# A decoder block's opening: x in rows with row sums of squares, the first modulation block shared by TensorE and VectorE, and the turned x loaded by pieces

## The chip, the core and the metric

The kernel runs on one core of a Trainium2 chip. The metric is the device time of one execution in microseconds (us). Five engines work side by side, each through its own instructions in a fixed order: TensorE (PE in the profile; its weight loads are PEld), VectorE (DVE), ScalarE (ACT), GpSimd (POOL) and SyncE (SP), which here only issues DMAs. An instruction that waits for another engine or for a DMA holds up everything behind it on its own engine.

## The reference

The reference is one decoder block on 256 rows of width 2048, in float32. Only its beginning matters here:

```python
ada = c @ w_ada + b_ada                      # c (1, 2048), w_ada (2048, 6144)
shift, scale, gate = jnp.split(ada, 3, axis=-1)
h = rms_norm(x, g_pre) * (1.0 + scale[:, None, :]) + shift[:, None, :]
proj = h @ w_in                              # w_in (2048, 11824)
```

`rms_norm` divides each row of x by the root of its mean square (plus 1e-6) and multiplies by g_pre. After that come two attention mixers on slices of `proj`, two branch products, a merge, an output product, a second norm with `gate`, and the residual sum. All of that is the same in both kernels.

## The kernel before

**The products.** Activations are kept turned: width on partitions, rows of x along the free axis. The width of 2048 falls into 16 blocks of 128, numbered kt. `h` is made piece by piece: block 0, blocks 1 to 2, 3 to 6, 7 to 9, 10 to 12 and 13 to 15. Pass 0 multiplies block 0 of h with its weights for 16 panels of `w_in` (8 items of two panels each, read in float32 by L564, the last two items by L560). Pass 1 takes blocks 1 and 2, pass 2 blocks 3 to 6, pass 3 the rest. From pass 1 on, a weight item is split into a high half `wH` (ACT, L520) and a low half `wL` (DVE, L521), and TensorE makes three products (L582, L584, L587).

**The modulation.** For block kt, shift and scale are sums of a column block of `w_ada` times c. `w_ss` holds those columns turned, so that output columns lie on partitions and the sum over the 2048 runs along the free axis. VectorE multiplies such a tile by `cB`, a copy of c on all partitions, and adds up along the row: L194 in eight halves for block 0, L529 in 1024-wide items for the others. `cB` is copied out of `c_ps`, four products of a column of ones with c in one row (L142).

**The norm.** `xs` holds the turned x (four DMAs of 512 KB). ACT squares it (L172, L179), GpSimd adds two halves (L173), VectorE squares a last part (L181), and TensorE sums over partitions with 40 matmul instructions on a column of ones (L186). From the sums, `rsqrt` makes `rstd`; L225 spreads it over all partitions into `rB_ps`, ACT copies that to `rstdB`. Block 0 is `x0` (L260), then `hF` (L283). GpSimd multiplies the other 15 blocks of `xs` by `rstdB` into `xT` (L751, five instructions), and `make_h` reads them.

**Order.** `items` is one list of weight items and modulation items. SP issues their DMAs in that order (`dma`, L501) into a ring of 7 buffers `raw`, each of 512 KB; a buffer is issued again once its reader is done. The first four buffers hold block 0's modulation weights. `keep_warm` (L135) issues matmuls whose results nobody reads. `behind` sets an instruction after another in the scheduler's order; the rest of each engine's order is the scheduler's, fixed when the kernel is built.

Of the kernel before, what the change touches and what calls it, by code (L numbers as in the profile page):

```python
# [9 lines left out]
F32 = mybir.dt.float32  # L10
# [40 lines left out]
def _build(ctx, tc, d_in, out):  # L51
# [39 lines left out]
    crow = ST[0:1, 2:4].rearrange("p a n -> p (a n)")  # L91
    pos_i = const.tile([128, 3], I32)
    A.dma_start(crow, d_in["c"])
    for q in range(4):
        DMA.dma_start(xs[:, 4 * q:4 * q + 4, :], d_in["xT"][:, 4 * q:4 * q + 4, :])
# [53 lines left out]
    i_mask = finish_mask_b()

    def c_halves():
        for j in (1, 3):
            last = A.activation(cB[:, j // 2, 512:1024], c_ps[j], AF.Copy)
        return last


    raws0 = []
    for q in range(4):
        r = wp.tile([128, 2, 512], F32, name="raw0", tag="raw", bufs=RAW)
        for half in range(2):  # L160
            DMA.dma_start(r[:, half], d_in["w_ss"][0, :, half, q * 512:(q + 1) * 512])
        raws0.append(r)

    last_sq = []
    ss_ps = psum.tile([128, NT, 2], F32, name="ss_ps", tag="pt")
    for q in range(4):
        if q % 2 == 0:
            sqs = big.tile([128, 2, 1024], F32, name="sqs", tag=("za", "zb")[q // 2])
        sq, xq = sqs[:, q % 2], xs[:, 4 * q:4 * q + 4, :].rearrange("p k s -> p (k s)")
        if q < 3:  # L170
            with behind(*last_sq):
                last_sq = [A.activation(sq, xq, AF.Square)]  # L172
            G.tensor_tensor(sq[:, 0:512], sq[:, 0:512], sq[:, 512:1024], op=OP.add)  # L173
            if q == 0:
                with behind(*last_sq):
                    last_sq = [c_halves()]
        else:
            with behind(*last_sq):
                A.activation(sq[:, 0:512], xq[:, 0:512], AF.Square)  # L179
            with behind(i_cV, i_mask):  # L180
                i_sq = V.tensor_tensor(sq[:, 512:1024], xq[:, 512:1024], xq[:, 512:1024], op=OP.mult)  # L181
        nk = 2 if q < 3 else 4
        for k in range(nk):
            for t in range(NT):
                with behind(i_warm):
                    i_ss = T.matmul(ss_ps[:, t, 0:1], lhsT=sq[:, k * S + t * 128:k * S + (t + 1) * 128],  # L186
                                    rhs=ones[:, 0:1], start=(q == 0 and k == 0 and t == 0),
                                    stop=(q == 3 and k == nk - 1), skip_group_check=True)
    sums0 = const.tile([128, 2, 5], F32)

    def sum0(q, half, after):
        r = raws0[q][:, half]
        with behind(after):
            return V.scalar_tensor_tensor(r, r, 1.0, cB[:, q // 2, q % 2 * 512:(q % 2 + 1) * 512], op0=OP.mult,  # L194
                                          op1=OP.mult, accum_out=sums0[:, half, q:q + 1])

    with behind(i_sq):
        V.tensor_copy(sums0[:, 0, 4:5], bT[:, 0, 0:1])
        i_sum = V.tensor_scalar(sums0[:, 1, 4:5], bT[:, 1, 0:1], 1.0, None, op0=OP.add)
    for q in range(2):  # L200
        for half in range(2):
            i_sum = sum0(q, half, i_sum)
    ssq = const.tile([128, NT], F32)
    with behind(i_sum):
        i_ssq = V.tensor_scalar(ssq, ss_ps[:, :, 0], 1.0 / D, EPS, op0=OP.mult, op1=OP.add)
    i_sum = sum0(2, 0, i_ssq)
# [16 lines left out]
    rB_ps = psum.tile([128, S], F32, name="rB_ps", tag="pv")  # L223
    for t in range(NT):
        i_rB = T.matmul(rB_ps[:, t * 128:(t + 1) * 128], lhsT=rstd[:, t:t + 1].to_broadcast([128, 128]), rhs=ident,  # L225
                        start=True, stop=True)
# [5 lines left out]
    A.activation(rstdB, rB_ps, AF.Copy)  # L232

# [26 lines left out]
    V.scalar_tensor_tensor(x0, xs[:, 0], gT[:, 0:1], rB_ps, op0=OP.mult, op1=OP.mult)  # L260

# [5 lines left out]
    def make_h(a, b):  # L267
        n = b - a
        if a:
            V.tensor_tensor(AB[:, :, a:b], sums[:, :, a:b, 0], bT[:, :, a:b], op=OP.add)  # L270
            V.tensor_tensor(AB[:, :, a:b], sums[:, :, a:b, 1], AB[:, :, a:b], op=OP.add)
            V.scalar_tensor_tensor(AB[:, 1, a:b], AB[:, 1, a:b], 1.0, gT[:, a:b], op0=OP.add, op1=OP.mult)
            h = ST[:, 2 + len(hxn) % 2].rearrange("p (k s) -> p k s", k=4)
        else:
            V.tensor_reduce(AB[:, :, 0], sums0, axis=AX.X, op=OP.add)
            h = hF
        hxn.append(a)
        for kt in range(a, b):
            src = xT[a][:, kt - a] if a else x0
            if a >= PASSES[2][0]:  # L280
                A.activation(h[:, kt - a], src, AF.Identity, scale=AB[:, 1, kt:kt + 1], bias=AB[:, 0, kt:kt + 1])
            else:
                V.tensor_scalar(h[:, kt - a], src, AB[:, 1, kt:kt + 1], AB[:, 0, kt:kt + 1], op0=OP.mult, op1=OP.add)  # L283
        ia = A.activation(xH[:, a:b], h[:, :n], AF.Copy)
        low = lows(a, b, "xL", F32R)
        iv = V.tensor_tensor(low, h[:, :n], xH[:, a:b].bitcast(F32), op=OP.subtract)
        xL.put(low, a, b)
        return ia, iv
# [143 lines left out]
    def ada_items(piece):  # L432
        a, b = piece
        res = []
        for kt in range(a, b):
            for half in range(2):
                for q in range(2):
                    it = Item()
                    it.kind, it.piece, it.kt0, it.half, it.q, it.nk, it.n = "ada", piece, kt, half, q, 1, 1024
                    it.src = d_in["w_ss"][kt, :, half, q * 1024:(q + 1) * 1024]  # L440
# [66 lines left out]
    def prep(i):  # L507
# [239 lines left out]
    def side_main():  # L747

        for a, b in groups[1:]:
            xT[a] = lows(a, b, "xT", F32)  # L750
            G.tensor_tensor(xT[a], xs[:, a:b, :], rstdB[:, None, :].to_broadcast([128, b - a, S]), op=OP.mult)  # L751
            yield
# [507 lines left out]
def _laid_out(v):  # L1260
# [43 lines left out]
```

## Time and profile before

| | |
|---|---|
| median of 3 runs | 815.86 us (814.46 to 819.72) |
| profiled execution | 814.65 us; its span 812.9 us, so 1.75 us lie around the span |
| granted TensorE clock over the span, mean | 0.989 |
| busy share of the span | PE 98%, DVE 83%, ACT 54%, POOL 11% |
| first product of pass 0 (L564) | starts at 23.87 us |
| first product of pass 1 (L582) | starts at 55.03 us |

Times in the views count from the start of the span. A row of the timeline reads: start, duration, engine, line, operation, output<-inputs, shapes, count, and in brackets the idle time before it with what ended that. Durations of PE instructions overlap, since matmuls are pipelined; the spacing of starts is their cost. The chain of waits gives start, duration, engine, tile, line. Each row of the table by windows gives the busy time of each engine, then the granted TensorE clock (1.00 is full), the share of the 16 DMA engines and GB/s.

### The profile page before, as it was taken

The page shows a single profiled execution, that of the slowest core. Times are in us where ns is not written, and L with a number is a line of the kernel's source. Part 1 is how long each engine was busy: PE and PEld are TensorE (multiplying, and loading weights), DVE is VectorE, ACT ScalarE, POOL GpSimd, SP SyncE. Part 2 cuts the span into 40 slices and gives each one's busy share as a digit, 9 for nine tenths or more (in the row PEclk, how much of TensorE's full clock was granted, in tenths as well). Part 3 has the DMA queues.
Part 4 walks back from the last instruction along what each step waited for, and adds up shares of the span by engine and source line. Part 5 has one row for each costly group of instructions (what it writes and reads, how often), then busy time and mean ns, then how long its engine had stood idle before and what let it go on. Part 6 is the DMA issues. An engine that isn't in the chain of part 4 may idle for free.

```text
span 812.9 us, 11775 instructions
## 1 busy us (share of the span) xinstructions
PE 795.0 (98%) x4125; PEld 663.7 (82%) x4125; DVE 671.2 (83%) x1074; ACT 441.3 (54%) x722; POOL 90.8 (11%) x109
## 2 busy tenths in 40 slices
PE   8989999999999999999999999999999999999995
PEld 5467988889888889888778999888888888888884
DVE  6969989999995979898788997869886888867465
ACT  3564673444444656576776767655644344445451
POOL 2500000000000026044311211002100000000000
PEclk8999999999999999999999999999999999999998
DMA  8699989999896557635334334657688889976632
GB/s 327 205 355 327 325 316 324 370 319 353 267 393 215 189 197 252 214 129 160 126 118 136 127 117 155 206 178 225 219 269 307 301 298 323 304 220 234 208 101 103
DMA packets 57088, 193.24 MB, mean 238 GB/s; under 512 B 6595, under 2 KB 7491, under 8 KB 56645
## 3 DMA queue, kind: packets, MB, share of 16 engines
q1 hardware_dynamic: 56160, 189.16, 68.1%
q10 hardware_dynamic: 870, 3.34, 1.2%
q8 instruction: 32, 0.52, 0.3%
q14 instruction: 26, 0.21, 0.1%
HBM read 190.38 MB, written 2.10 MB: 237 GB/s over the span
## 4 chain that ended last, share of the span: by engine, by line
PE 93%; DVE 3%; issue 1%; ACT 1%; DMA 1%; POOL 0%; DVEq 0%; ACTq 0%
PE mm L582 23%; PE mm L587 23%; PE mm L584 23%; PE mm L577 3%; PE mm L572 3%; PE mm L574 3%; PE mm L564 2%; PE pt_ps L959 1%; PE sA L923 1%; PE warm L135 1%; PE mm L560 1%; DMA raw<-in_weights_dram 1%; DVE wL L521 1%; PE pvb_ps L1100 1%; PE sB L1090 1%
## 5 line engine op out<-in xcount | busy, mean ns | idle before, releaser
L520 ACT ACTIVATE wH<-raw 128x1024 fp32r<-128x1024 f32 (+2 forms) x268 | 267.3, 1000 | 270.1 <-PE mm L584 215.3
L521 DVE TENSOR_TENSOR wL<-raw,wH 128x1024 fp32r<-128x1024 f32 (+2 forms) x268 | 316.1, 1183 | 89.6 <-ACT wH L520 85.0
L582 PE MATMUL mm<-wH,xH 128*128 128x512 f32 (+2 forms) x616 | 237.1, 387 | 0.8 <-DVE K L677 0.4
L584 PE MATMUL mm<-wH,xL 128*128 128x512 f32 (+2 forms) x616 | 234.3, 382 | 0.0
L587 PE MATMUL mm<-wL,xH 128*128 128x512 f32 (+2 forms) x616 | 188.1, 382 | 0.0
L582 PEld LDWEIGHTS mm<-wH,xH 128*128 128x128 f32 x616 | 115.8, 188 | 22.3 <-issue 1.0
L587 PEld LDWEIGHTS mm<-wL,xH 128*128 128x128 f32 x616 | 113.8, 188 | 22.5 <-DVE wL L521 0.3
L584 PEld LDWEIGHTS mm<-wH,xL 128*128 128x128 f32 x616 | 115.9, 188 | 19.9
L529 DVE SCALAR_TENSOR_TENSOR raw<-raw,ST 128x1024 f32<-128x1024 f32 x60 | 77.4, 1299 | 3.6 <-DMA raw<-in_w_ss_dram 3.6
L572 PE MATMUL mm<-xH,wH 128*128 128x256 f32 x240 | 62.4, 280 | 0.0
L574 PE MATMUL mm<-xL,wH 128*128 128x256 f32 x240 | 62.2, 280 | 0.0
L582 PE MATMUL mm<-wH,yH 128*128 128x512 f32 x128 | 50.4, 394 | 0.0
L582 PE MATMUL mm<-wH,mH 128*128 128x512 f32 x128 | 50.1, 391 | 0.0
L584 PE MATMUL mm<-wH,yL 128*128 128x512 f32 x128 | 49.9, 390 | 0.0
L584 PE MATMUL mm<-wH,mL 128*128 128x512 f32 x128 | 49.9, 390 | 0.0
L577 PE MATMUL mm<-xH,wL 128*128 128x256 f32 x240 | 49.0, 280 | 0.0
L572 PEld LDWEIGHTS mm<-xH,wH 128*128 128x128 f32 x240 | 45.0, 188 | 0.1
L574 PEld LDWEIGHTS mm<-xL,wH 128*128 128x128 f32 x240 | 45.0, 188 | 0.1
L533 DVE SCALAR_TENSOR_TENSOR gacc<-raw,small,gacc 128x1024 f32<-128x1024 f32 x32 | 40.9, 1278 | 0.0
L587 PE MATMUL mm<-wL,mH 128*128 128x512 f32 x128 | 39.8, 389 | 0.0
L587 PE MATMUL mm<-wL,yH 128*128 128x512 f32 x128 | 39.5, 390 | 0.0
L954 POOL TENSOR_TENSOR P<-P,cf 128x512 f32<-128x512 f32 x24 | 27.1, 1128 | 94.6 <-DVE cf L952 51.7
(294 smaller groups left out, 1021.5 us busy)
## 6 DMA issues: line engine op xcount, KB each, us to landing
raw<-in_weights_dram SPq DMA_DIRECT2D x237, 512.0 KB, 4.6
raw<-in_w_ss_dram SPq DMA_DIRECT2D x60, 512.0 KB, 5.6
raw<-in_w_gate_dram SPq DMA_DIRECT2D x32, 512.0 KB, 5.2
raw<-in_weights_dram SPq DMA_DIRECT2D x29, 256.0 KB, 3.4
raw<-in_weights_dram SPq DMA_DIRECT2D x7, 304.0 KB, 3.8
xs<-in_xT_dram SPq DMA_DIRECT2D x4, 512.0 KB, 4.9
raw<-in_w_ss_dram SPq DMA_DIRECT2D x8, 256.0 KB, 6.1
xr<-in_x_dram ACTq DMA_DIRECT2D x2, 1024.0 KB, 8.7
```

The source lines that it names most:

```text
L520: highest[0] = A.activation(H, raw, AF.Copy)
L521: lowest[0] = V.tensor_tensor(L, raw, H.bitcast(F32), op=OP.subtract)
L529: V.scalar_tensor_tensor(r, r, 1.0, cB[:, it.q], op0=OP.mult, op1=OP.mult, accum_out=sums[:, it.half, it.kt0, it.q:it.q + 1])
L533: V.scalar_tensor_tensor(acc, raw[:, 0, :], cT[:, it.kt0:it.kt0 + 1], acc, op0=OP.mult, op1=OP.add)
L564: T.matmul(job.ps[t][:, :job.n], lhsT=hj[:, t * 128:(t + 1) * 128], rhs=it.raw[:, j, cs], start=(first and j == 0), stop=(last and j == it ...
L572: T.matmul(ps, lhsT=it.H[:, j, bs], rhs=sH[:, it.kt0 + j, :], start=(first and j == 0 and b == 0), stop=False, skip_group_check=True)
L574: T.matmul(ps, lhsT=it.H[:, j, bs], rhs=sL[:, it.kt0 + j, :], start=False, stop=False, skip_group_check=True)
L577: T.matmul(ps, lhsT=it.L[:, j, bs], rhs=sH[:, it.kt0 + j, :], start=False, stop=(last and j == it.nk - 1), skip_group_check=True)
L582: T.matmul(ps, lhsT=sH[:, it.kt0 + j, ts], rhs=it.H[:, j, cs], start=(first and j == 0), stop=False, skip_group_check=t in job.seeded)
L584: T.matmul(ps, lhsT=sL[:, it.kt0 + j, ts], rhs=it.H[:, j, cs], start=False, stop=False, skip_group_check=t in job.seeded)
L587: T.matmul(ps, lhsT=sH[:, it.kt0 + j, ts], rhs=it.L[:, j, cs], start=False, stop=(last and j == it.nk - 1), skip_group_check=t in job.seeded)
L954: G.tensor_tensor(pv, pv, cf[:, :u.nb, None].to_broadcast([128, u.nb, u.len]), op=OP.mult)
```

## The change

- `xs` now holds x itself, 128 rows on partitions, two halves of 1024 columns for each of two row tiles. The squares are summed along the row by the instruction that squares: ACT takes three parts (L165, L174, L175), DVE two (L168). The 40 summing matmuls, GpSimd's sums and 20 warming matmuls go; the 8 warming matmuls at the start stay.
- c is no longer loaded as a row. `c_ps` is made by 16 products of a spread column of c with the identity matrix, each 128x128 (L154).
- `w_first` holds block 0's columns of `w_ada` in rows (the summed 2048 on partitions in 16 blocks, 256 columns for shift and scale). Eight of the 16 blocks are multiplied by TensorE into `ada_ps` (L186, two products each), eight are added up by VectorE in `acc0`, a part of the tile `lead` (L192, 256 wide). `acc0` starts from `diag`, the bias on a diagonal. Two last products with ones (L242) add `acc0` into `ada_ps`; `hF` (L287) reads shift and scale there.
- Block 0 of the turned x is a DMA of 128 KB. The other pieces are loaded, one DMA each (L510), into `xT` just ahead of the first modulation item of their piece, and VectorE multiplies them in place by `rstdB` (L541), at the first modulation item of the piece's last block. GpSimd's L751 is gone.

```diff
-    xs = big.tile([128, KT, S], F32, name="xs", tag="ma")
+    xs = big.tile([128, NT, D], F32, name="xs", tag="ma")
-    A.dma_start(crow, d_in["c"])
-    for q in range(4):
-        DMA.dma_start(xs[:, 4 * q:4 * q + 4, :], d_in["xT"][:, 4 * q:4 * q + 4, :])
     A.dma_start(small, d_in["small"])
     A.dma_start(pos_i, d_in["pos"])
+    for t in range(NT):
+        for v in range(2):
+            sl = slice(v * 1024, (v + 1) * 1024)
+            DMA.dma_start(xs[:, t, sl], d_in["x"][t * 128:(t + 1) * 128, sl])
+    for q in range(4):
+        r = wp.tile([128, 4, 2, 128], F32, name="raw0", tag="raw", bufs=RAW)
+        for v in range(2):
+            sl = slice(4 * q + 2 * v, 4 * q + 2 * v + 2)
+            DMA.dma_start(r[:, 2 * v:2 * v + 2], d_in["w_first"][:, sl])
+            if q == 0 and v == 0:
+                DMA.dma_start(x0T, d_in["xT"][:, 0, :])
...
-            i_c = T.matmul(ps, lhsT=ones[0:1, :], rhs=crow[:, j * 512:(j + 1) * 512], start=True, stop=True)
+            for v in range(4):
+                i_c = T.matmul(ps[:, v * 128:(v + 1) * 128], rhs=ident, start=True, stop=True,
+                               lhsT=cT[:, 4 * j + v:4 * j + v + 1].to_broadcast([128, 128]))
-    with behind(i_c):
-        i_warm = keep_warm(6)
...
+    A.activation(junk[0], xs[:, 0, 0:1024], AF.Square, accum_out=ssp[:, 0:1])
+    def square(t, a, b, slot):
+        return V.scalar_tensor_tensor(junk[1][:, :b - a], xs[:, t, a:b], 1.0, xs[:, t, a:b], op0=OP.mult, op1=OP.mult,
+                                      accum_out=ssp[:, slot:slot + 1])
+    i_sq = square(0, 1024, 2048, 1)
...
+    def ada0_part(kt, first=False):
+        for half in range(2):
+            last = T.matmul(ada0[:, half], lhsT=raws0[kt // 4][:, kt % 4, half],
+                            rhs=cT[:, kt:kt + 1].to_broadcast([128, 128]),
+                            start=(first and half == 0), stop=False, skip_group_check=True)
+        return last
+    def ada0_sum(kt, first=False):
+        return V.scalar_tensor_tensor(acc0, raws0[kt // 4][:, kt % 4], cT[:, kt:kt + 1], diag if first else acc0,
+                                      op0=OP.mult, op1=OP.add)
+    on_pe, on_dve = (0, 2, 4, 6, 8, 10, 12), (1, 3, 5, 7, 9, 11, 13, 14)
...
-    with behind(i_ss):
-        keep_warm(8)
-    with behind(i_rB):
-        keep_warm(6)
...
+        if n == 3:
+            with behind(i_sum):
+                i_sum = V.tensor_tensor(x0, x0, rB_ps, op=OP.mult)
+            T.matmul(ada0[:, half], lhsT=acc0[:, half], rhs=ones, start=False, stop=True, skip_group_check=True)
...
+            V.tensor_scalar(h[:, 0], x0, ada0[:, 1, 0:1], ada0[:, 0, 0:1], op0=OP.mult, op1=OP.add)
...
+        if it.kind == "ada" and it.new:
+            a, b = it.piece
+            xT[a] = lows(a, b, "xT", F32)
+            DMA.dma_start(xT[a], d_in["xT"][:, a:b, :])
...
+                if it.scaled:
+                    xn = xT[it.piece[0]]
+                    V.tensor_tensor(xn, xn, rstdB[:, None, :].to_broadcast([128, xn.shape[1], S]), op=OP.mult)
...
-        for a, b in groups[1:]:
-            xT[a] = lows(a, b, "xT", F32)
-            G.tensor_tensor(xT[a], xs[:, a:b, :], rstdB[:, None, :].to_broadcast([128, b - a, S]), op=OP.mult)
-            yield
```

Three places show what the change does to the order. The first is the start of VectorE's program. `ident` and `identb` are the identity matrix, which the warming matmuls wait for; L168 is a square of x's second half, L177 the sum of two partial sums, one of them from ACT. Before:

```order
L79 MEMSET ones_f 128x128
L99 MEMSET one 128x1
L81 CAST ones_r<-ones_f 128x128
L73 TENSOR_SCALAR ident<-diff 128x128
L77 TENSOR_SCALAR causal<-diff 128x128
L75 CAST identb<-ident 128x128
```

Now:

```order
L79 MEMSET ones_f 128x128
L110 MEMSET one 128x1
L81 CAST ones_r<-ones_f 128x128
L168 SCALAR_TENSOR_TENSOR ST,ssp<-xs 128x1024
L177 TENSOR_TENSOR ssq<-ssp 128x1
L73 TENSOR_SCALAR ident<-diff 128x128
L77 TENSOR_SCALAR causal<-diff 128x128
L75 CAST identb<-ident 128x128
```

The square and the sum now stand ahead of the identity matrix. The second place is VectorE's program around `hF`, block 0 of h. Before:

```order
L194 SCALAR_TENSOR_TENSOR raw_145,sums_184<-raw_145,ST 128x512
L194 SCALAR_TENSOR_TENSOR raw_148,sums_184<-raw_148,ST 128x512 x2
L260 SCALAR_TENSOR_TENSOR ST<-xs,small,rB_ps 128x256
L275 TENSOR_REDUCE AB<-sums_184 128x2
L283 TENSOR_SCALAR hF<-ST,AB 128x256
L286 TENSOR_TENSOR xL_261<-hF,xH 128x256
```

Now (`xT_237` is the piece of blocks 1 and 2):

```order
L192 SCALAR_TENSOR_TENSOR lead<-raw_101,small,lead 128x256
L237 TENSOR_TENSOR lead<-lead,rB_ps 128x256
L192 SCALAR_TENSOR_TENSOR lead<-raw_101,small,lead 128x256
L192 SCALAR_TENSOR_TENSOR lead<-raw_104,small,lead 128x256 x2
L541 TENSOR_TENSOR xT_237<-xT_237,rstdB 128x512
L287 TENSOR_SCALAR hF<-lead,ada_ps 128x256
L291 TENSOR_TENSOR xL_251<-hF,xH 128x256
```

Three sums of block 0 follow the product with `rB_ps`, and the first piece's scaling stands ahead of `hF`. The third place is ACT's program at the end of pass 0, where it copies results out of PSUM (`VB`, `ZA`, `ZB`) and makes the first high halves `wH` for pass 1. Before:

```order
L675 ACTIVATE VB<-mm 128x512 x3
L520 ACTIVATE wH<-raw 128x1024
L675 ACTIVATE ZA<-mm 128x512 x3
L520 ACTIVATE wH<-raw 128x1024
L675 ACTIVATE ZA<-mm 128x512
L675 ACTIVATE ZB<-mm 128x512 x2
```

Now:

```order
L689 ACTIVATE VB<-mm 128x512
L322 ACT_TABLE_LOAD
L322 ACTIVATE sin_t<-ang 128x72
L531 ACTIVATE wH<-raw 128x1024
L323 ACTIVATE cos_t<-ang 128x72
L689 ACTIVATE ZA<-mm 128x512 x4
L689 ACTIVATE ZB<-mm 128x512 x2
L616 ACTIVATE mm<-CV 128x512
L689 ACTIVATE ZB<-mm 128x512
L531 ACTIVATE wH<-raw 128x1024
```

The table load with the sines has come forward from pass 1, and the second `wH` now stands behind the third copy to `ZB` instead of the third to `ZA`.

More of the change, by code (lines that the diff above doesn't have):

```diff
@@ L115, in _build @@
         V.tensor_scalar(mf, mi, 0.0, None, op0=OP.is_equal)
-        i_mask = V.tensor_tensor(multB, multB, mf, op=OP.add)
+        V.tensor_tensor(multB, multB, mf, op=OP.add)
     def finish_mask_b():
@@ L149, in _build @@
[L149 to L206, printed above, removed]
+    diag = diag.rearrange("p (h k) -> p h k", h=2)
+    V.tensor_scalar(diag[:, 0], ident, bT[:, 0, 0:1], None, op0=OP.mult)
+    V.scalar_tensor_tensor(diag[:, 1], ident, bT[:, 1, 0:1], ident, op0=OP.mult, op1=OP.add)
@@ new lines, in _build @@
+    ssq = const.tile([128, NT], F32)
+    ssp = const.tile([128, 5], F32)
+    junk = [ST[:, 2], ST[:, 3]]
+    A.activation(junk[0], xs[:, 0, 0:1024], AF.Square, accum_out=ssp[:, 0:1])
[3 more added lines that the diff above has]
+    i_sq = square(0, 1024, 2048, 1)
+    with behind(i_sq):
+        finish_mask_b()
+    A.activation(junk[0], xs[:, 1, 0:1024], AF.Square, accum_out=ssp[:, 2:3])
@@ new lines, in _build @@
+    i_sqA = A.activation(junk[0][:, 0:512], xs[:, 1, 1024:1536], AF.Square, accum_out=ssp[:, 3:4])
+    i_sq = square(1, 1536, 2048, 4)
+    V.tensor_tensor(ssq[:, 0:1], ssp[:, 0:1], ssp[:, 1:2], op=OP.add)
+    V.tensor_reduce(ssq[:, 1:2], ssp[:, 2:5], axis=AX.X, op=OP.add)
+    i_ssq = V.tensor_scalar(ssq, ssq, 1.0 / D, EPS, op0=OP.mult, op1=OP.add)
+    ada0 = psum.tile([128, 2, 128], F32, name="ada0_ps", tag="pv")
+    acc0 = acc0.rearrange("p (h k) -> p h k", h=2)
+    def ada0_part(kt, first=False):
[4 more added lines that the diff above has]
+        return last
@@ L208, in rsqrt @@
+    def ada0_sum(kt, first=False):
+        return V.scalar_tensor_tensor(acc0, raws0[kt // 4][:, kt % 4], cT[:, kt:kt + 1], diag if first else acc0,
+                                      op0=OP.mult, op1=OP.add)
+    on_pe, on_dve = (0, 2, 4, 6, 8, 10, 12), (1, 3, 5, 7, 9, 11, 13, 14)
+    with behind(i_c):
+        for kt in on_pe[:3]:
+            i_ada = ada0_part(kt, kt == 0)
+    with behind(i_ssq):
+        i_sum = ada0_sum(on_dve[0], True)
     def rsqrt(dst, ms, name):
@@ L222, in _build @@
         i_sum = rsqrt(rstd, ssq, "x")
[L223 to L226, printed above, removed]
-    with behind(i_ss):
-        keep_warm(8)
-    with behind(i_rB):
-        keep_warm(6)
+    with behind(tab["root"]):
+        for j in range(4):
+            A.activation(cB[:, j // 2, j % 2 * 512:(j % 2 + 1) * 512], c_ps[j], AF.Copy)
+    with behind(i_sqA):
+        A.activation(x0, x0T, AF.Copy, scale=gT[:, 0:1])
+    rB_ps = psum.tile([128, S], F32, name="rB_ps", tag="pt")
+    with behind(i_ada):
+        for t in range(NT):
+            i_rB = T.matmul(rB_ps[:, t * 128:(t + 1) * 128], lhsT=rstd[:, t:t + 1].to_broadcast([128, 128]), rhs=ident,
+                            start=True, stop=True)
     rstdB = const.tile([128, S], F32)
     A.activation(rstdB, rB_ps, AF.Copy)
+    with behind(i_rB):
+        for kt in on_pe[3:]:
+            i_ada = ada0_part(kt)
+    for n, kt in enumerate(on_dve[1:]):
+        with behind(i_sum):
+            i_sum = ada0_sum(kt)
+        if n == 3:
+            with behind(i_sum):
+                i_sum = V.tensor_tensor(x0, x0, rB_ps, op=OP.mult)
+    with behind(i_ada):
+        i_ada = ada0_part(KT - 1)
+    with behind(i_ada):
+        for half in range(2):
+            T.matmul(ada0[:, half], lhsT=acc0[:, half], rhs=ones, start=False, stop=True, skip_group_check=True)
     xH = big.tile([128, KT, S], F32R, name="xH")
@@ L439, in ada_items @@
                     it.kind, it.piece, it.kt0, it.half, it.q, it.nk, it.n = "ada", piece, kt, half, q, 1, 1024
-                    it.src = d_in["w_ss"][kt, :, half, q * 1024:(q + 1) * 1024]
+                    it.src = d_in["w_ss"][kt - 1, :, half, q * 1024:(q + 1) * 1024]
+                    it.new = kt == a and half == 0 and q == 0
+                    it.scaled = kt == b - 1 and half == 0 and q == 0
                     it.fin = kt == b - 1 and half == 1 and q == 1
```

35 lines of the change are left out of this document (16 added, 19 removed).

## The prediction

> **What bounds the kernel now.** I read the chain of waits first. The page gives its shares, the chain by time its opening.
>
> ```profile
> PE 93%; DVE 3%; issue 1%; ACT 1%; DMA 1%; POOL 0%; DVEq 0%; ACTq 0%
> ```
> ```profile
> 1.85 3.60 PE warm L135 x8
> ...
> 18.04 3.01 PE warm L135 x7
> 21.05 0.85 PE rB_ps L225 x4
> 21.90 2.02 PE warm L135 x7
> 23.93 12.24 PE mm L564 x32
> 36.17 6.81 DMA raw<-in_weights_dram
> 43.11 5.37 PE mm L564 x8
> 48.48 6.91 PE mm L560 x32
> ```
>
> TensorE carries the span, so only what lets its products start earlier or run without a gap counts. The table by windows shows where they do not, for the lead-in, pass 0, the first part of pass 1, and the long stretch behind it:
>
> ```profile
> 0.00:23.87 23.87, 21.69 (x80) 12.20 (x81) 16.20 (x46) 6.75 (x11) 7.28 (x14) 0.79 0.84 309
> 23.87:55.03 31.16, 28.07 (x81) 15.48 (x81) 25.53 (x71) 20.10 (x38) 9.77 (x5) 0.95 0.77 268
> 55.03:80.00 24.97, 24.22 (x115) 19.59 (x113) 23.56 (x42) 13.60 (x19) 0.00 (x0) 1.00 0.92 340
> 80.00:240.00 160.00, 160.00 (x864) 139.19 (x865) 151.81 (x215) 80.61 (x97) 0.00 (x0) 1.00 0.92 332
> ```
>
> From 80 us TensorE is never idle, and the change leaves its products there alone: what is won or lost before 80 us is the result. Pass 0 has two gaps, here with what ended them:
>
> ```profile
> 37.17 3.67 PE L564 MATMUL mm<-raw,hF 128*128 128x512 f32 x8 [0.82 <-DMA raw<-in_weights_dram]
> 43.11 5.37 PE L564 MATMUL mm<-raw,hF 128*128 128x512 f32 x8 [2.27 <-DMA raw<-in_weights_dram]
> ```
>
> The item behind the second gap also takes 5.37 us where the one before took 3.67: 0.82 + 2.27 + 1.70 = 4.8 us lost. The weights were late because their buffers were. In the groups from 22 to 36 us, from 36 to 60 us, and the waits of SP's queue up to 60 us:
>
> ```profile
> L751 POOL TENSOR_TENSOR xT<-xs,rstdB 128x768 f32<-128x768 f32 (+2 forms) x5 | 11.1, 2246 | 8.2 <-ACT rstdB L232 8.2
> L529 DVE SCALAR_TENSOR_TENSOR raw<-raw,ST 128x1024 f32<-128x1024 f32 x4 | 9.5, 2421 | 0.0
> L529 DVE SCALAR_TENSOR_TENSOR raw<-raw,ST 128x1024 f32<-128x1024 f32 x7 | 8.5, 1220 | 2.0 <-DMA raw<-in_w_ss_dram 2.0
> SPq L501 <- DVE raw L529: 15.1, 7, 7.2
> ```
>
> VectorE needs 2421 ns for a modulation item while GpSimd scales xT, and 1220 ns after. SP waits 15.1 us for these items, once 7.2 us.
>
> **The lead-in.** The new order puts a square of x's second half ahead of the identity matrix. When does that half land? Issues on SP, their landing (the second row is the middle of the first two), and the identity matrix and the last mask today:
>
> ```profile
> 1.18 0.90 SPq L95 DMA_DIRECT2D xs<-in_xT_dram  x2
> xs<-in_xT_dram SPq DMA_DIRECT2D x1, 512.0 KB, 3.9
> xs<-in_xT_dram SPq DMA_DIRECT2D x2, 512.0 KB, 4.4
> 1.17 0.23 DVE L73 TENSOR_SCALAR ident<-diff 128x128 f32<-128x128 int32 x1
> 5.60 0.26 DVE L121 TENSOR_SCALAR maskB<-multB 128x384 bf16<-128x384 bf16 x1
> ```
>
> The second transfer takes 2 x 4.4 - 3.9 = 4.9 us from 1.18, so it lands at 6.1. The square costs a 1024-wide 1.22, with its sum 7.4; `ident` goes from 1.17 to 7.5, and the warming matmuls from 1.85 to 8.1. They end at 11.7 (3.60 as now).
>
> Then TensorE runs the new small products. In instructions, two for each float32 product, as the two `rB_ps` products are four now: 32 for `c_ps`, 12 for the first three blocks of `ada_ps`, 4 for `rB_ps`, 20 for the other five, 4 for the last sums. No such chain is in the trace; these are the nearest rows, `rB_ps` in the chain above, a later 128x128 group in the chain, and the clock by windows of TensorE alone (start and end, length, busy time, clock):
>
> ```profile
> 558.14 0.89 PE pvb_ps L1100 x8
> 16.00:17.80 1.80, 1.80 (x11) 0.50 1.02 407
> 20.80:21.80 1.00, 1.00 (x6) 0.50 0.49 119
> ```
>
> At the full clock one is 0.89 / 8 = 0.111 us, at half 0.85 / 4 = 0.2125. So 72 instructions cost 8.0 or 15.3 us. I take the full clock, since the warming matmuls come just before, with 0.8 us extra until it has stepped up. `rB_ps` is then done at 11.7 + 0.8 + 48 x 0.111 = 17.8. Its `rstd` isn't late: behind the square at 7.4 stand on VectorE the identity and masks (4.7 us from 1.17 to 5.86 today), the second square (0.7) and small instructions (I take 1.6), which end near 14.4. Behind it stand, by these rows, ACT's copy, the product with `rB_ps`, a 256-wide instruction (two here) and a 512-wide one:
>
> ```profile
> 21.94 0.38 ACT L232 ACTIVATE rstdB<-rB_ps 128x256 f32<-128x256 f32 x1 [3.46 <-PE rB_ps L225]
> 22.36 0.48 DVE L260 SCALAR_TENSOR_TENSOR ST<-xs,small,rB_ps 128x256 f32<-128x256 f32 x1 [0.94 <-ACT rstdB L232]
> 46.05 0.73 DVE L283 TENSOR_SCALAR ST<-xT,AB 128x256 f32<-128x256 f32 x2
> 47.48 0.69 DVE L286 TENSOR_TENSOR xL<-ST,xH 128x512 fp32r<-128x512 f32 x1 [0.70 <-ACT xH L284]
> ```
>
> 0.4 + 0.5, three dependent sums at 0.4, the scaling of `xT` 0.7 (beside it the last sums on TensorE, 0.44), `hF` 0.4, some 0.3 of handover: L564 starts at 21.3 instead of 23.87, **2.6 us earlier**. Against the clock at half it is 27.6, against one at full from 8.1 on 18.7: the ends. The scaling waits for a DMA. The first weight item's issue and its time to landing today:
>
> ```profile
> 9.93 0.33 SPq L501 DMA_DIRECT2D raw<-in_weights_dram  x1
> raw<-in_weights_dram SPq DMA_DIRECT2D x1, 512.0 KB, 6.2
> ```
>
> It lands at 16.1, behind as many bytes as in the new order; `xT_237` follows 0.75 MB later, at the 309 GB/s above 18.6, before the 20.1 at which it is needed.
>
> [...] The rows: TensorE was busy all 1.80 us of 16.00 to 17.80, in one-column sums, and its clock stood at 0.50. [...]
>
> **Pass 0.** Without GpSimd's work VectorE's modulation items take 1.22, and the first starts 1.1 us behind `hF`. It frees its buffer at 23.7, for the fourth weight item. That is needed after two full items (3.43 each) and a short one of 560 columns (1.95; three full and one short are the 12.24 of the chain), at 30.1. With the longest landing in the chain, 6.8, it comes at 30.5. The fifth (issued 25) and the sixth (29, as SP keeps its order behind a wait for the second weight item) come by 31.8 and 35.8, needed at 33.5 and 36.9. So the gaps go, and with them **4.8 us**. Late next would be h of blocks 1 and 2, ready near 39, needed at 47.7. What could spoil it: the four modulation buffers of block 0 come free only as TensorE and VectorE finish with them, between 17 and 21 by the times above, which costs cover, not yet a wait. GpSimd's 11.1 us were hidden and bring nothing by themselves.
>
> **Pass 1.** The third place of the order has a price. Today's rows of the second `wH` and its `wL`, the table load, the sixth item's `wL`, what TensorE waited for behind it, a 768-wide VectorE instruction, and one of ACT's copies in pass 0 with its idle time:
>
> ```profile
> 51.60 1.05 ACT L520 ACTIVATE wH<-raw 128x1024 fp32r<-128x1024 f32 x1
> 52.68 1.22 DVE L521 TENSOR_TENSOR wL<-raw,wH 128x1024 fp32r<-128x1024 f32 x1 [0.22 <-ACT wH L520]
> 59.50 1.28 ACT L317 ACT_TABLE_LOAD   x1
> 67.19 0.78 DVE L521 TENSOR_TENSOR wL<-raw,wH 128x608 fp32r<-128x608 f32 x1
> 69.83 0.48 PE L582 MATMUL mm<-wH,xH 128*128 128x512 f32 x1 [0.41 <-DVE K L677]
> 165.83 0.95 DVE L286 TENSOR_TENSOR xL<-ST,xH 128x768 fp32r<-128x768 f32 x1
> 35.53 0.60 ACT L675 ACTIVATE QB<-mm 128x512 f32<-128x512 f32 x1 [0.26 <-PE mm L564]
> ```
>
> The table load, ahead of the copies to `ZA`, holds TensorE's PSUM banks: 1.28 less the slack of 0.26 between copies at three banks, **0.5 us**. The second `wH` moves from 3.4 us before the start of pass 1 (55.03) to that start, because it now stands behind the third copy to `ZB`. Its `wL` begins 1.0 after the start instead of 2.4 before. From there to the end of the sixth item's `wL` VectorE has 13.7 us of work as now: three splits and four modulation items at 1.14 apiece, nine evacuations for 4.3, two short splits 1.4. It ends 14.7 after the start; today it is 67.97, 12.9 after. Today's margin is nothing, as the 0.41 wait right behind shows, so the lag of **1.8 us** falls on TensorE. Its lower end is 0 (VectorE catches up), its upper end 3.4. The 1024-wide scaling (1.2) fits in VectorE's wait for that `wH`.
>
> The other three scalings are 768 wide, 0.95 each by a 768-wide `xL` later on. Beside them VectorE is 151.81 of 160 us busy and TensorE never waits: I cost them at nothing, hidden in the three weight items that are split ahead. Without that cover it is 2.9 us. The new DMAs are 1.9 MB, under 1% of the 193 MB; SP issues each where it waits for a buffer anyway.
>
> **Sum.** -2.6 - 4.8 + 0.5 + 1.8 = -5.1 us, for the profiled execution 814.65 - 5.1 = 809.6. The median of the runs lies 1.2 above that execution, within their spread; I leave the forecast at **809.6 us**, 0.8% below the median.
>
> **Rivals.**
> - *The small products run at the half clock* (the slower side). For it: the clock rows, and that TensorE stands still until 8.1. Against: these products fill all 128 rows and columns, and 3.6 us of dense matmuls lead them. L564 then starts at 27.6 (+3.7), and pass 0's first items are still slow for two products' worth of doubled time (1.7). In all +3.7 + 1.7 - 4.8 + 0.5 + 1.8 = +2.9: 817.6. It becomes slower than before once the half clock lasts some 10 us beyond 12.5.
> - *Pass 0 still waits for its weights*, because the buffers of block 0 come free late and SP's order keeps the weights behind modulation items. For it: a margin of -0.4 to 1.7 by the longest landing. Against: the DMA engines carry only 0.77 in pass 0 now. The change then doesn't remove what it could; 3 to 4.8 us come back: 812.6 to 814.4. An unhidden scaling (+2.9: 812.5) lands in the same place.
> - *VectorE isn't late in pass 1* (its spans overlap, so "busy" overstates): no 1.8, no 0.5, and the clock full at once: 806.
>
> **Chances.** Forecast, 806.8 to 812: 0.50. Half clock: 0.17. Waits remain or scalings show: 0.15. No lag: 0.18. The range 804.8 to 816.6 leaves out about a tenth on each side: the better end of the last rival, the worse half of the first. A measurement of this kernel tells 1% from no change, 8.2 us. Faster by more, below 807.7, are most of the no-lag case and the forecast's lower end: 0.23. Slower by more would take 824: 0.03. Within: 0.74.
>
> **What would show it.** `warm` starting near 8 and `rB_ps` near 17; the granted clock 1.00 from 13 us on; L564 at 21.3, without a wait for `raw`; modulation items at 1220 ns from the first; pass 1 near 48 us; a wait of TensorE for `wL` within its first 15 us. Wrong would be a clock of 0.50 at 16 to 24 us, a bracket with DMA in pass 0, or `ident` not waiting for x.

## The result and the profile after

The changed kernel takes 809.88 us in the median of 6 runs (809.57 to 810.53), the kernel before 818.23 us (814.46 to 820.28): a ratio of 0.9904, 95% interval 0.9876 to 0.9932. The profiled execution went from 814.65 to 809.57 us. The forecast was 809.6.

First the chain of waits of the changed kernel, its shares by engine:

```profile
PE 91%; DVE 4%; ACT 2%; issue 2%; DMA 1%; DVEq 0%; SPq 0%; ACTq 0%
```

TensorE still carries the span. The table by windows has lead-in, pass 0, the first part of pass 1, and the stretch from 80 us:

```profile
0.00:21.35 21.35, 11.92 (x81) 9.56 (x81) 12.34 (x41) 8.06 (x16) 1.16 (x9) 1.00 0.90 337
21.35:48.00 26.65, 26.11 (x81) 15.03 (x81) 18.47 (x71) 20.71 (x40) 0.15 (x1) 1.00 0.94 361
48.00:80.00 32.00, 29.90 (x138) 23.99 (x137) 30.62 (x48) 16.78 (x22) 0.00 (x0) 1.00 0.90 311
80.00:240.00 160.00, 160.00 (x866) 139.40 (x865) 152.74 (x219) 78.01 (x94) 0.00 (x0) 1.00 0.93 336
```

Lead-in 21.35 us (23.87 before), pass 0 26.65 (31.16), its DMA share 0.94 (0.77); from 80 us nothing is changed. Now the timeline of TensorE, lead-in and pass 0, then the places where it waits:

```profile
8.73 3.60 PE L146 MATMUL warm<-identb 128*128 128x512 bf16 x8 [8.73 <-DVE identb L75]
12.12 3.80 PE L154 MATMUL c_ps<-ident,small 128*128 128x128 f32 x32
15.76 1.50 PE L186 MATMUL ada_ps<-small,raw 128*128 128x128 f32 x12
17.10 0.61 PE L225 MATMUL rB_ps<-ident,rstd 128*128 128x128 f32 x4
21.35 19.29 PE L578 MATMUL mm<-raw,hF 128*128 128x512 f32 x48 [0.56 <-issue]
44.63 3.72 PE L574 MATMUL mm<-hF,raw 128*128 128x256 f32 x16 [0.54 <-ACT ZA L689]
48.00 0.58 PE L596 MATMUL mm<-wH,xH 128*128 128x512 f32 x1
61.93 0.38 PE L596 MATMUL mm<-wH,xH 128*128 128x304 f32 x1 [1.11 <-DVE QA L693]
64.70 0.47 PE L596 MATMUL mm<-wH,xH 128*128 128x512 f32 x1 [0.73 <-DVE K L691]
```

No row of L578 waits for a DMA: the 0.82 and 2.27 us and the slow item are gone. The wait at 64.70 stands where the one at 69.83 stood, so the profiled execution is 5.13 us ahead there, and 5.08 at its end. In pass 1, from 48.00 on, VectorE begins the second `wL` at 49.38:

```profile
49.38 1.23 DVE L532 TENSOR_TENSOR wL<-raw,wH 128x1024 fp32r<-128x1024 f32 x1 [1.65 <-ACT wH L531]
```

The modulation items in the groups from 22 to 36 us, and SP's waits for them up to 60 us:

```profile
L543 DVE SCALAR_TENSOR_TENSOR raw<-raw,ST 128x1024 f32<-128x1024 f32 x7 | 8.6, 1223 | 1.9 <-DMA raw<-in_w_ss_dram 1.7
```
```profile
SPq L512 <- DVE raw L543: 3.1, 4, 0.8
```

1223 ns from the first item on instead of 2421, and 3.1 us of waiting instead of 15.1.

One thing was not in the forecast: the medians are 8.3 us apart, not the 5.1 of the two profiles. Runs of the kernel before differ by 6 us, those of the changed one by 1.0. Where that comes from, the last part of the experiments shows.

### The profile page after: what moved, and what is told of

It reads as the page before. It is cut to its first block, busy times and chain, and to the rows that moved or that the text cites. A ratio compares the mean times of both kernels' runs of the same rounds, so it can differ in the third digit from the quotient of the medians.

```text
span 807.8 us, 11760 instructions
## 1 busy us (share of the span) xinstructions
PE 783.6 (97%) x4125; PEld 660.6 (82%) x4125; DVE 665.2 (82%) x1073; ACT 442.4 (55%) x727; POOL 75.2 (9%) x101
## 4 chain that ended last, share of the span: by engine, by line
PE 91%; DVE 4%; ACT 2%; issue 2%; DMA 1%; DVEq 0%; SPq 0%; ACTq 0%
PE mm L601 23%; PE mm L596 23%; PE mm L598 22%; PE mm L591 3%; PE mm L588 3%; PE mm L586 3%; PE mm L578 2%; PE pt_ps L969 1%; DVE wL L532 1%; PE sA L933 1%; DMA xs<-in_x_dram 1%; PE pvb_ps L1110 1%; PE sB L1100 1%; ACT wH L531 1%; PE ot_ps L991 1%
## 5 line engine op out<-in xcount | busy, mean ns | idle before, releaser
L543 DVE SCALAR_TENSOR_TENSOR raw<-raw,ST 128x1024 f32<-128x1024 f32 x60 | 72.8, 1218 | 2.9 <-DMA raw<-in_w_ss_dram 2.8
L591 PEld LDWEIGHTS mm<-xH,wL 128*128 128x128 f32 x240 | 37.1, 188 | 0.0
```

Source lines behind the costliest of these rows:

```text
L543: V.scalar_tensor_tensor(r, r, 1.0, cB[:, it.q], op0=OP.mult, op1=OP.mult, accum_out=sums[:, it.half, it.kt0, it.q:it.q + 1])
L591: T.matmul(ps, lhsT=it.L[:, j, bs], rhs=sH[:, it.kt0 + j, :], start=False, stop=(last and j == it.nk - 1), skip_group_check=True)
```

## The experiments

The intervals of the ratios below are 0.24 to 0.36% wide on each side, 2.0 to 2.9 us, because the kernel before scatters. The runs of the changed kernel lie within 1.0 us and those of most variants within 0.4 to 1.5, so among them medians and traces are compared.

### What the pass-0 term rests on

**Only the scalings.** The kernel before, L751 on VectorE:

```diff
-            G.tensor_tensor(xT[a], xs[:, a:b, :], ...)
+            V.tensor_tensor(xT[a], xs[:, a:b, :], ...)
```

> The kernel before with one edit: its five scalings of turned x on VectorE instead of GpSimd. Theory (the prediction's pass-0 term): the modulation items that GpSimd slows beside itself hold the weight buffers, so without GpSimd the two idle stretches of pass 0 (0.82 and 2.27 us) and the slow item behind them (1.70) go, 3 to 4.8 us under the kernel before (about 814 against a median of 818). Rival: the buffers are late because the lead-in is, or because the weight transfers queue behind others; then the stretches stay and the time is that of the kernel before within 1 us. A third reading: what GpSimd slowed is off the path in most runs; then the profile shows items of 1.2 us and the same waits.

812.45 us (811.17 to 815.93), ratio 0.9936 (0.9904 to 0.9968); profiled 812.23. Its table by windows, the lead-in behind 8.4 us and pass 0:

```profile
8.40:25.70 17.30, 17.30 (x64) 12.15 (x63) 10.13 (x30) 3.59 (x6) 3.20 (x2) 0.51 0.79 291
26.19:52.02 25.83, 25.83 (x82) 15.06 (x81) 20.87 (x73) 19.05 (x36) 0.15 (x1) 1.00 0.86 311
```

And its modulation items in the groups of pass 0:

```profile
L529 DVE SCALAR_TENSOR_TENSOR raw<-raw,ST 128x1024 f32<-128x1024 f32 x9 | 10.8, 1222 | 2.1 <-DMA raw<-in_w_ss_dram 1.0 <-PE mm L564 1.0
```

The items take 1222 ns, and pass 0 takes 25.83 us instead of 31.16, without a wait, although it starts at 26.19, 2.3 us later than in the profile of before. The later start isn't what helps: an execution of the kernel before at 820.31 us, shown further down, starts pass 0 at 29.40, still waits 1.03 and 2.13 us for weights in it, and takes 30.11. The theory holds: the scalings alone bring 4.3 to 5.3 us in pass 0. In time, runs of like mean clock lie about 4 us under the kernel before of the same series (811.17 to 812.45 against 815.95 and 816.10, 815.33 and 815.93 against 818.34 to 820.60), which is the 3 to 4.8 expected.

**Only the rest.** The changed kernel, L541 on GpSimd:

```diff
-                    V.tensor_tensor(xn, xn, rstdB[:, None, :]...)
+                    G.tensor_tensor(xn, xn, rstdB[:, None, :]...)
```

> The changed kernel with its five scalings of xT on GpSimd instead of VectorE, at the same places. If GpSimd's work slows VectorE as it did before the change (2421 ns for a modulation item instead of 1220), VectorE gains its own 4.9 us and loses about as much again: the time within 1 us of the changed kernel, with modulation items near 2400 ns beside the scalings. If the scalings on VectorE are a load that pass 1 pays for, this version is 1 to 3 us faster.

811.55 us (811.39 to 812.56), ratio 0.9928 (0.9904 to 0.9952): 1.7 us above the changed kernel, where at most 1 was expected. Its timeline, GpSimd, VectorE, and TensorE's pass 0:

```profile
18.73 1.27 POOL L541 TENSOR_TENSOR xT<-xT,rstdB 128x512 f32<-128x512 f32 x1 [16.95 <-ACT rstdB L228]
43.34 2.35 POOL L541 TENSOR_TENSOR xT<-xT,rstdB 128x1024 f32<-128x1024 f32 x1 [23.34 <-DMA xT<-in_xT_dram]
19.02 2.30 DVE L192 SCALAR_TENSOR_TENSOR lead<-raw,small,lead 128x256 f32<-128x256 f32 x3
22.65 19.29 PE L578 MATMUL mm<-raw,hF 128*128 128x512 f32 x48 [0.56 <-issue]
```

Pass 0 has no wait for weights here either. GpSimd now scales each piece when it lands, so its work no longer stands as one block of 11.1 us beside the first modulation items: between these two rows it stands still for 23.34 us. It costs time in the lead-in: three sums take 2.30 us beside it instead of 1.52. Pass 0 starts 1.30 us later than in the changed kernel, at 22.65; 0.78 of that are the sums. The other 0.52 are no effect of the edit: the 32 products of `c_ps` ahead of it take 4.37 us from their start to the next row's, in the changed kernel's profile 3.64. So the pass-0 waits have two cures, VectorE for the scaling or the scaling by pieces, and the change has both. Neither comes on top of the other.

### What the lead-in waits for

**One warming matmul.** `keep_warm(8)` becomes `keep_warm(1)`.

> The changed kernel with one warming matmul instead of eight. If the small 128x128 products are dense enough to raise TensorE's clock by themselves, they begin near 9.1 at half speed, the clock steps up within 3 to 7 us, and L578 starts 1 to 2 us earlier: 808 to 809. If they are not (the first rival of the prediction), the 72 instructions run at 0.2125 us each, L578 starts near 25 and the time is 3 to 6 us longer.

809.10 us (808.65 to 809.15), ratio 0.9894 (0.9858 to 0.9930). TensorE in its timeline:

```profile
8.89 5.34 PE L154 MATMUL c_ps<-ident,small 128*128 128x128 f32 x32
19.65 15.86 PE L578 MATMUL mm<-raw,hF 128*128 128x512 f32 x40 [0.56 <-issue]
36.03 3.67 PE L578 MATMUL mm<-raw,hF 128*128 128x512 f32 x8 [0.52 <-DMA raw<-in_weights_dram]
```

The first rival (small products at the half clock) falls: behind one warming matmul the products of `c_ps` come to the full rate by themselves. The microseconds from 9 to 12 hold 7, 6 and 7 of TensorE's instructions, the next two 10 and 11, so the step comes near 12, about 3.5 us after TensorE's first matmul at 8.49. They take 5.34 us instead of 3.80, and pass 0 starts 1.70 earlier. About half of that is lost again, most of it to a wait for weights.

**The identity first.** The square is set behind the identity and the first masks:

```diff
-    i_sq = square(0, 1024, 2048, 1)
+    with behind(i_id, i_mask):
+        i_sq = square(0, 1024, 2048, 1)
```

> The changed kernel with the square of x's second half set behind the identity matrix and the first masks on VectorE; nothing else changes. If the late identity is what holds the lead-in (the changed kernel's TensorE stands still until 8.73 us), the warming matmuls start near 1.9, the spread of c follows when its DMA lands (6 to 7), and L578 of pass 0 starts near 19.2, held by the scaling of the first xT piece, which waits for its DMA (near 18) ahead of hF; 17 if that has landed by then. So 2 to 4 us less than the changed kernel's 809.9. If the lead-in is set by x's DMAs and the norm (rstd), nothing changes.

809.27 us (809.20 to 810.68), ratio 0.9902 (0.9871 to 0.9932): hardly anything. VectorE and TensorE in the timeline, and the table by windows around the start of pass 0 (all lines are one further down in this kernel):

```profile
18.04 0.69 DVE L542 TENSOR_TENSOR xT<-xT,rstdB 128x512 f32<-128x512 f32 x1 [2.20 <-DMA xT<-in_xT_dram]
19.16 20.99 PE L579 MATMUL mm<-raw,hF 128*128 128x512 f32 x48 [2.56 <-issue]
```
```profile
16.00:19.00 3.00, 0.61 (x4) 0.42 (x4) 0.96 (x2) 0.00 (x0) 0.00 (x0) 1.00 1.03 416
19.00:22.00 3.00, 2.83 (x4) 1.32 (x5) 2.52 (x7) 1.01 (x2) 0.00 (x0) 0.55 1.03 412
```

Pass 0 starts 2.19 us earlier, at 19.16 as expected, but its first 48 products take 20.99 us instead of 19.29, so the 2 to 4 us expected don't come. `hF` stands behind the scaling of the first piece (blocks 1 and 2), that behind a transfer which lands at 18.0; TensorE stands still for 2.56 us, and its clock is half for the first products.

**Both.** As above, and the scaling set behind `hF`: items 8 to 11 of the list now wait for h of block 0 too, and the scaling is among them.

```diff
-        with behind(*(first_h if i < 8 else ...
+        with behind(*(first_h if i < 12 else ...
```

> The early identity of the run before (square behind it), and the scaling of block 1's turned x behind h of block 0 instead of ahead of it. With the early identity alone h waited 2.2 us for that scaling's transfer, TensorE stood 2.56 us and began pass 0 at half clock (19.16, first four products doubled, 1.7 us lost). Theory: h of block 0 comes at about 17, TensorE stands under 1 us, the clock stays at 1.00, pass 0 starts at 17.2 instead of 21.35 in the changed kernel. What follows decides between two: if the weights come in time the end moves by 3.5 to 4 (806); if the transfers (1.0 of the engines' time from 5 us on) are the next bound, pass 0 waits for weights by 1 to 3 us, as the run with one warming matmul did by 0.52, and the end moves by 1 to 2 (808).

**806.57 us** (806.40 to 806.76), ratio 0.9846 (0.9822 to 0.9870), better than both kernels. TensorE in its timeline:

```profile
17.38 15.86 PE L579 MATMUL mm<-raw,hF 128*128 128x512 f32 x40 [0.56 <-issue]
33.45 3.67 PE L579 MATMUL mm<-raw,hF 128*128 128x512 f32 x8 [0.21 <-DMA raw<-in_weights_dram]
44.85 0.58 PE L597 MATMUL mm<-wH,xH 128*128 128x512 f32 x1
58.78 0.38 PE L597 MATMUL mm<-wH,xH 128*128 128x304 f32 x1 [1.09 <-DVE QA L694]
```

Pass 0 starts 3.97 us earlier at the full clock, pass 1 3.15 earlier; the end moves by 3.3. The transfers cost only 0.21 us of waiting, less than the 1 to 3 expected in the second case; the wait for ACT's copies to `ZA` at the end of pass 0 grows from 0.54 to 0.90.

### What pass 1's lag is worth

**The sines later.** 16 more steps ahead of the sines in the side work, the small instructions that the program places among the items:

```diff
+        for _ in range(16):
+            yield
         with behind(first_copy[0]):
             sines(angles)
```

> The changed kernel with the sines (and ACT's table load) 16 steps later in the side work; the scheduler then also puts the second wH ahead again, behind the second copy to ZA. If ACT's place of these is what made TensorE wait in pass 1 (0.54 us on a copy to ZA, then 1.1 and 0.7 us on VectorE), 1.5 us go, at least 0.5. If VectorE simply has too much work there (the 1024-wide scaling of xT among it), the waits stay within 0.3 us of what they are and the time is the same.

809.63 us (808.48 to 809.91), ratio 0.9899 (0.9869 to 0.9930): 0.25 under the changed kernel, less than the 0.5 expected at least. TensorE in its timeline has no wait at the place of the one at 44.63 any more. The first wait in pass 1 in the same view:

```profile
61.93 0.38 PE L596 MATMUL mm<-wH,xH 128*128 128x304 f32 x1 [1.10 <-DVE QA L693]
```

The 0.54 are the table load's, as forecast. Pass 0 starts 0.41 us later in this execution (at 21.76; its `c_ps` takes 4.10 us, again without an edit there), and pass 1 nevertheless 0.39 earlier, at 47.61. But the waits at 61.93 and 64.70 stand at the same times, so VectorE's lag takes the 0.39 back. The second `wH` stands behind the fourth copy to `ZB` in this kernel (48.49; 48.30 in the changed one) and not ahead, as the expectation had it, so whether its place makes the lag isn't tested here.

**Fewer modulation items at its start.**

```diff
-    items += spread(ws, pieces(1), 0.8)
+    items += spread(ws, pieces(1), 0.8, 3)
```

> The changed kernel with pass 1's modulation items spread behind its third weight item instead of from the first on. Theory (the prediction's 1.8): VectorE has no slack in the first 15 us of pass 1; without two or three items of 1.14 there, TensorE's waits of 1.11 and 0.73 us at 61.9 and 64.7 go, and the time falls by 1.5 to 1.8, to about 808.2. Rival: the lag is only moved, since the same items come closer together later in pass 1, where VectorE is as full; then TensorE waits there and the time stays at 809.5 to 810. Second rival: weights land too late for pass 1's first items; then the waits stay where they are, with a transfer as their end.

810.05 us (809.45 to 810.59), ratio 0.9890 (0.9861 to 0.9920). Both waits of pass 1 are gone from TensorE's timeline, and there are new ones:

```profile
46.15 2.86 PE L574 MATMUL mm<-hF,raw 128*128 128x256 f32 x12 [0.30 <-ACT ZA L689]
82.09 0.38 PE L586 MATMUL mm<-xH,wH 128*128 128x256 f32 x1 [0.62 <-ACT mm L616]
240.83 0.73 PE L601 MATMUL mm<-wL,xH 128*128 128x512 f32 x2 [0.63 <-DVE wL L532]
```

1.84 us go, 1.55 come back at these three places, one a wait for VectorE and two for ACT, and the profiled span is 807.8 as before. So the lag can be moved, but nothing is won; the first rival holds in the time, and in part in its reason (VectorE carries 152.74 of 160 us behind 80 us in the changed kernel). What removed the two waits stays open: with fewer items at the start, the second and third `wH` also come ahead of pass 1, at 44.56 and 46.94 instead of 48.30 and 49.73.

**Both passes, on top of the best kernel.**

```diff
-    items += spread(ws, pieces(0), 0.75, 1)
+    items += spread(ws, pieces(0), 1.0, 1)
```

and the edit above it, in the kernel of 806.57 us.

> The same with the modulation items of passes 0 and 1 spread later (pass 0 over all its weight items instead of three quarters, pass 1 behind its third). Theory (transfers bound pass 0, VectorE pass 1): a weight item comes one or two transfers of 1.3 us earlier, so pass 0 waits less than in the run beside it, and the 1.8 of pass 1 go: 1.5 to 3 us under that run, about 805. Rival: h of blocks 1 and 2 is then too late, needed near 44 and ready near 45: pass 1 starts 1 to 2 us late and the time is that of the run beside it or worse.

808.17 us (807.27 to 810.78), ratio 0.9871 (0.9842 to 0.9901): worse than without. The rival holds. Pass 1 in its timeline, and the windows behind its start:

```profile
45.70 1.20 PE L597 MATMUL mm<-wH,xH 128*128 128x512 f32 x4 [2.30 <-ACT xH L290]
```
```profile
47.50:50.50 3.00, 3.00 (x8) 2.33 (x8) 2.47 (x5) 0.00 (x0) 0.00 (x0) 0.50 0.82 240
```

h of blocks 1 and 2 comes 2.30 us late, and in this execution the wait costs a second time, through 3.4 us at half clock. It is the slowest of the four (810.78); whether the other three, 807.27 to 808.38, pay the second time is not shown.

### Why the kernel before scatters

Over its 42 runs beside the experiments, 21 lie from 813.31 to 817.21 us with a mean granted clock of 0.984 to 0.991, and 21 from 818.34 to 822.53 with 0.993 to 0.998. The slower ones show the higher clock. All runs of the changed kernel show 0.996 to 0.998.

**The kernel before, profiled again.**

> The kernel before, unchanged, for a second profile. Its runs fall into two groups: about 816 with a mean granted clock of 0.988, and about 819.6 with 0.997; the profile that the prediction was worked out from (814.65, clock 0.989) is of the first. [...]

> The same once more, so that at least one execution of the group at 819.6 is likely to be profiled; expectation as in the run beside it.

The first took 820.31 us. The second took 1132.29, with a granted clock of 0.64 or 0.65 in every stretch; nothing here rests on it. The first one's products in the timeline, and its lead-in in the table by windows:

```profile
5.38 7.19 PE L142 MATMUL c_ps<-ST,ones_r 1*128 1x512 f32 x8
15.04 8.53 PE L186 MATMUL ss_ps<-ones_r,sqs 128*128 128x1 f32 x40
29.40 12.48 PE L564 MATMUL mm<-raw,hF 128*128 128x512 f32 x32
48.71 3.67 PE L564 MATMUL mm<-raw,hF 128*128 128x512 f32 x8 [2.13 <-DMA raw<-in_weights_dram]
59.51 0.58 PE L582 MATMUL mm<-wH,xH 128*128 128x512 f32 x1
```
```profile
5.38:27.20 21.82, 21.82 (x66) 13.94 (x66) 8.26 (x29) 4.36 (x7) 4.32 (x5) 1.00 0.70 259
```

And the same products in the execution of 814.65 us, with three of its windows:

```profile
5.38 3.86 PE L142 MATMUL c_ps<-ST,ones_r 1*128 1x512 f32 x8
11.70 2.26 PE L186 MATMUL ss_ps<-ones_r,sqs 128*128 128x1 f32 x16
14.29 3.75 PE L186 MATMUL ss_ps<-ones_r,sqs 128*128 128x1 f32 x24 [0.32 <-POOL sqs L173]
```
```profile
9.20:12.50 3.30, 3.30 (x12) 1.83 (x11) 3.08 (x8) 3.01 (x4) 1.60 (x1) 0.50 1.01 364
12.60:15.90 3.30, 2.98 (x27) 2.90 (x27) 2.19 (x4) 0.00 (x0) 1.63 (x1) 1.00 1.05 408
16.05:22.70 6.65, 6.65 (x24) 4.29 (x24) 3.61 (x15) 0.59 (x2) 0.30 (x1) 0.50 0.74 270
```

The eight passes over one row take 7.19 us instead of 3.86: TensorE runs at half rate from the start to about 27 us, though it is always busy and the granted clock reads 1.00, as it does in each microsecond up to 56, so this half rate is not in that row. The 814.65 execution had the full rate from the one-row products on, and its drops are what lowers its mean clock. So by this execution, and by the mean clocks of the other runs, the upper group is the one that never got going: it pays 5.53 us in the lead-in (29.40 against 23.87). Pass 0 is 1.05 shorter than in the 814.65 execution and the stretch from there to the wait at 75.53 (69.83 there) 1.22 longer: together 5.70, against 5.66 by the times. Against the changed kernel the numbers are: lead-in -8.05, pass 0 30.11 to 26.65, -3.46, from there to the wait at 75.53 (64.70 after) +0.68: -10.83, by the times -10.74. So it is not that everything behind 60 us is slower and the lead-in the same. The kernel with the old lead-in and the scalings on VectorE has the same two groups (811.17 to 812.45 at 0.987 to 0.990, 815.33 and 815.93 at 0.997), so GpSimd's scalings don't make them; the lead-in is what the two kernels share and the changed one lacks.

**One row again, in the changed kernel.** c is loaded as a row as before and spread by four products:

```diff
-            for v in range(4):
-                i_c = T.matmul(ps[:, v * 128:(v + 1) * 128], rhs=ident, ...
-                               lhsT=cT[:, 4 * j + v:4 * j + v + 1].to_broadcast([128, 128]))
+            i_c = T.matmul(ps, lhsT=ones[0:1, :], rhs=crow[:, j * 512:(j + 1) * 512], ...)
```

> The changed kernel with c spread as the kernel before did it: four products of one row (c as a row of 512) instead of 32 of 128 rows. [...]

814.92 us, ratio 0.9967 (0.9938 to 0.9996). The two groups are back: 4 runs from 811.61 to 812.57 (clock 0.993 or 0.994), 6 from 814.87 to 815.37 (0.997). TensorE in the timeline of one of the six:

```profile
11.78 7.19 PE L155 MATMUL c_ps<-crow,ones_r 1*128 1x512 f32 x8
18.90 2.93 PE L186 MATMUL ada_ps<-small,raw 128*128 128x128 f32 x12
26.75 19.29 PE L578 MATMUL mm<-raw,hF 128*128 128x512 f32 x48 [0.56 <-issue]
```

Only the products for `c_ps` and the load of c differ, and pass 0 starts 5.40 us later: `c_ps` takes 7.19 us instead of 3.80, and the first 12 products behind it 2.93 instead of 1.50. The one-row products fill TensorE's time and yet don't bring the full rate: in this execution it comes near 24 us, 12 us after their start. What the four faster runs do differently is not shown, as none of them was profiled.

**A longer warm-up before.** 16 warming matmuls instead of 8 at the start of the kernel before.

> The kernel before with 16 warming matmuls at the start instead of 8. Its two groups of runs differ from the first thin product on: in the execution at 820.31 its eight one-row passes took 7.19 us instead of 3.86 and its one-column sums 8.53 instead of about 6, so TensorE never came to full rate before 27 us, though the granted clock reads 1.00 there. [...]

820.03 us (817.23 to 821.56), ratio 1.0020 (0.9996 to 1.0045): no faster than with 8. From its table by windows, start and the stretch behind it:

```profile
1.85:10.20 8.35, 8.35 (x21) 3.17 (x22) 4.45 (x11) 2.75 (x4) 1.45 (x3) 1.00 0.95 329
10.30:27.60 17.30, 17.30 (x62) 12.04 (x61) 7.13 (x26) 3.49 (x6) 2.87 (x2) 0.51 0.60 228
```

No run shows 0.997 any more (0.984 to 0.989), so by this sign every run reaches the full rate. The time does not follow: the one-row and one-column products come behind, and the clock reads 0.51 over the 17.3 us from 10.3 on. In this lead-in a warm-up ahead of such products doesn't keep the rate for them.

## Why the prediction was right, and where it was not

- **Lead-in, -2.6 forecast, -2.52 measured.** L578 starts at 21.35 (forecast 21.3), `rB_ps` is done at 17.71 (17.8). Two steps are off and cancel: the warming matmuls start at 8.73 instead of 8.1, and the 0.8 for the clock's step, a guess that no run shows as the cost of a step, was 0.1 (32 instructions at 0.114). The second is luck of the profiled execution: the same 32 take 3.64 us in it, and 4.06, 4.10 and 4.37 in the profiles of three variants that don't touch them (fewer modulation items, the sines later, scalings on GpSimd). The changed kernel's runs lie in two narrow groups as well, 809.57 to 809.72 us with a mean clock of 0.998, the profiled one among them, and 810.04 to 810.53 with 0.996; whether this step parts them isn't shown.
- **Pass 0, -4.8 and +0.5 forecast, -4.51 together.** The waits and the slow item are gone, and the table load shows as the 0.54 at 44.63. The cause, VectorE beside GpSimd, is shown by the run with the scalings alone. The 2421 ns that the prediction reads as the price beside GpSimd are a mean of four: three items took 2.82 or 2.83 us up to 34.6, while GpSimd worked until 33.5, and the one behind them 1.21. What the text left out is that scaling x piece by piece as it lands would have done it too, on GpSimd.
- **Pass 1, +1.8 forecast, +1.90 measured.** (64.70 - 48.00 against 69.83 - 55.03.) The steps fit too: the second `wL` begins 1.4 us after the start of pass 1 (forecast 1.0), and the sixth item's ends 15.1 after it (14.7). That TensorE waits for VectorE there is shown; that the late second `wH` is the reason is the prediction's argument, and no run moves it alone. Against the execution at 820.31 the stretch is only 0.68 longer, because that one waits 1.15 us in it itself. Spreading pass 1's modulation items later brought nothing back.
- **Hidden scalings, 0 forecast.** Behind 80 us TensorE is busy 160.00 of 160.00 us. The three later scalings are hidden there. The first had little cover: with an identity 7 us earlier it is what `hF` waits for.
- **The rivals.** Half clock for the small products: falls for these products (one warming matmul is enough). The row that spoke for it, TensorE busy with the clock at 0.50, tells of one-column products. There (0.50 over the 6.65 us from 16.05), and for one-row products (7.19 us for eight with one row again), the fear was right, and the change removes both. Pass 0 still waiting for weights: not here; 0.52 us of it appear once pass 0 starts 1.7 earlier, 0.21 in the best kernel. VectorE not late: falls.
- **The step that failed** is the sentence on the median: 1.2 above the profiled execution, "within their spread". The spread was two groups, of which only the lower had been profiled. The changed kernel's 809.88 is right because it has lost them, yet the gain, 8.3 us between medians, is 5 against the lower group and 10 against the upper. Nothing in the prediction's sum says that the scatter would go, so the forecast was right in its time by the sum and by luck in leaving the 1.2 out. A profile of each group would have shown it; the three times given (814.46, 815.86, 819.72) only hinted at it.

## What to carry to other kernels

Where TensorE's small products lie ahead of everything else, make them fill rows and columns, even at more instructions: behind the same warm-up, 32 full ones cost 3.6 to 4.4 us here and keep the rate, 8 passes over one row cost 3.9 or 7.2 and lose it for what follows or never get it. Before a gain is put down to an edit, look whether the runs of the kernel before fall into groups, and profile one of each. A start made earlier is worth what the next wait leaves of it: here the order of one scaling decided between 0.6 and 3.3 us.

## What the runs showed of the hardware

- The granted clock's row read 1.00 over 21.82 us in which TensorE's products ran at half rate (the kernel before at 820.31: eight one-row passes in 7.19 us). In the first 30 us the spacing of starts is the measure.
- Being busy wasn't enough for the full rate: TensorE was busy for 21.82 of 21.82 us of one-row and one-column products with some warming matmuls among them, and the eight one-row passes took 7.19 us where another execution took 3.86. That other execution read 0.50 from 9.16, 15.99 and 43.29 us on, for 3.4, 6.8 and 3.4 us; with the identity first, and with both passes' items later, such a stretch lasted 3.4 us too. Why one execution of the same kernel has the full rate early and another doesn't, no run shows.
- Behind an idle stretch of 2.27 to 2.56 us the clock went to 0.50 (before, and the runs with the identity first and with both passes' items later); behind one of 0.54 to 1.11 it did not, nor behind one of 2.13 in the execution at 820.31 or of 2.17 in the run with 16 warming matmuls. No run shows whether the length alone decides.
